# A hybrid decoder step on one core: background loads issued by GpSimd, and a planner that counts eight transfers in flight

## Chip, core and metric

The kernel runs on one core of one Trainium2 chip, as one launch. The metric is the device time of that launch in microseconds (us). GB/s and MB are decimal, KB are 1024 bytes.

## The reference, cut to what matters

A prompt of 512 positions and eight sample sequences of 8 positions (64 rows) run through the same two layers; all data are float32.

```python
# layer 0: attention and short convolution
hn = rms_norm(x, g)
q, k, v, z_a, gate_b, gate_c, h_in, z_b = split(hn @ w_in_ab, 8)      # 2048 -> 8192
o_a = dilated_attn(rotary(q), rotary(k), v) * silu(z_a)               # 8 heads of 128; the sample rows
                                                                      # read a cache of 2048 positions
o_b = gate_b * conv3(gate_c * h_in) * silu(z_b)
x = x + concat(o_a, o_b) @ w_out_ab
# layer 1: diagonal complex state space, 128 groups of 16 channels and 64 states
u, z = split(rms_norm(x, g) @ w_in_c, 2)
y = gelu(s5_scan(u, h0, lam, step, B, C) + d_skip * u)
y = y * sigmoid(y @ w_glu + b_glu) * silu(z)
x = x + y @ w_out_c
return rms_norm(x, final_norm), new keys, values, conv and state-space states
```

## The kernel before, in words

**The matrix products.** The 576 rows of activations stay in SBUF as two tiles, a_hi and a_lo, whose sum is the float32 value. A product is 120 jobs: 64 jobs of 128 output columns for w_in_ab (24 for the q, k and v of the heads, 8 for z_a, 32 for the convolution), 4 wide jobs of 512 columns for w_out_ab, 32 for w_in_c, 16 for w_glu, 4 wide ones for w_out_c. The weights come in halves of 512 KB (tile w, `load_half`, three buffers). ACT rounds a quarter of a half into wh, DVE takes the difference wl, and TensorE (PE) adds a_hi*wh, a_lo*wh and a_hi*wl into the PSUM tile mm.

**The background.** Beside the jobs run threads, which are Python generators: the turning of x into a_hi and a_lo (`x_turn`, `x_split`, `x_rows`), the prompt's attention (`prompt_head`), the tables of the state space (`ssm_setup`, `ssm_x`, `ssm_c`), the attention of the sample rows (`far_load`, `sample_far`, `near_load`, `sample_near`), the scan of layer 1, the stores and reloads between stages, and the final norm with the rows of h read again (`h_again`). In `ssm_x` the tiles E8 and B8 (512 KB each, one buffer each) are read from DRAM and DVE makes X8 of them (the trace names them E, B and X); `ssm_c` reads small rows of C (tile cn) and makes the tables Cs. In the sample's attention the near cache rows and all value rows come through tile kv (six buffers), the far key rows through tile kf (three buffers), 512 KB each; DVE multiplies kf by the query row qr and sums into fs, from which E is made that PE turns (tile tf). (Tile E of the sample's attention and tile E8 of the tables share a short name in the trace; the stretch tells them apart.)

**What sets the order.** All engines execute in program order, and that order is laid down when the program is built. A planner (`Clock`) keeps an estimated time for each engine and for each tile, from costs written into `Clock.op` and `Clock.cost`. Between two steps of a job, `between` calls `step`, which lets every background thread that is ready by these estimates (`could`) emit one piece of its instructions; a thread names the engine and the tiles that it waits for with `W(...)`. Loads are emitted in the same manner: a transfer stands in the queue of the engine that issues it (SP, ACT or POOL), behind whatever that engine was given earlier. Each transfer ends on one of eight counters, taken in turn: SP and ACT share one set of eight, POOL has another, and a transfer whose counter is still in use waits for that earlier one. In the kernel before, all weight loads and nearly all background loads stand on SP; POOL has the stores of intermediate results, a few fills and copies, and two of the five small rows of vr. The planner's cost of a transfer knows nothing of the eight counters.

Nearly every instruction is recorded by the helper `Engine`, so the trace gives line L215 for all of them (L218 after the change) and the tiles tell them apart.

Of the kernel before, what the change touches and what calls it, by code (L numbers as in the profile page):

```python
# [78 lines left out]
class Clock:  # L79


    def __init__(self):
        self.t = {e: 0.0 for e in ("PE", "ACT", "DVE", "POOL", "SP")}
        self.port = self.base = 0.0
        self.dma = 6500.0
        self.exact = False
        self.wr, self.rd = {}, {}
        self.row, self.ring, self.born, self.gone = {}, {}, {}, set()
        self.last = {}
        self.sbuf = set()  # L90
# [80 lines left out]
    def op(self, eng, op, a, k):  # L171
# [107 lines left out]
def hybrid_step(tc, I, O):  # L279
# [156 lines left out]
    def step():  # L436
        evacs()
        for _ in range(1):
            again = False
# [283 lines left out]
    ACT.dma_start(out=vr[48:64], in_=I["final_norm"].rearrange("(r p) -> r p", p=P))  # L723
    ACT.dma_start(out=vr[64:88], in_=I["conv_w"][0].rearrange("i (r p) -> (i r) p", p=P))
    POOL.memset(dr4, 0.0)
    POOL.memset(ssq, 1.0)

    def load_consts():
        SP.dma_start(out=cosr, in_=I["c_cos"])
        SP.dma_start(out=sinr, in_=I["c_sin"])  # L730
        SP.dma_start(out=sr, in_=I["state_conv"][0].rearrange("b i f -> (b i) f"))
        SP.dma_start(out=dr4[:, :, 0:GC], in_=I["d_skip"][0].rearrange("(q gi k) -> q gi k", gi=4, k=GC))
        SP.dma_start(out=pmask, in_=I["c_pmask"])
        SP.dma_start(out=fmask, in_=I["c_fmask"])
        SP.dma_start(out=eye, in_=I["c_eye"])

# [456 lines left out]
    def ssm_x(sp):  # L1193
        for c in range(G // CH):
            g0 = c * CH
            yield W("SP", e_scr, b_scr, slot=[(sp, "E8", 1), (sp, "B8", 1)])
            E = sp.tile([P, CH, 2, ST], F32, name="E8", tag="E8", bufs=1)
            B = sp.tile([P, CH, 2, ST], F32, name="B8", tag="B8", bufs=1)
            SP.dma_start(out=E.rearrange("p g a s -> p (g a s)"), in_=e_scr[:, g0:g0 + CH, :]
                         .rearrange("t g p -> t (g p)").unsqueeze(1).to_broadcast([T, GC, CH * P]))  # L1200
            SP.dma_start(out=B.rearrange("p g a s -> p (g a s)"), in_=b_scr[:, g0:g0 + CH, :]
                         .rearrange("k g p -> k (g p)").unsqueeze(0).to_broadcast([T, GC, CH * P]))
# [3 lines left out]
            for a, (p, q, f) in enumerate(((br, bi, sub), (bi, br, add))):  # L1206
# [11 lines left out]
    def ssm_c(sp, B0, PWT):  # L1218
# [3 lines left out]
        def load_cn(c):  # L1222
            if c < G // CH:
                g0 = c * CH
                x = cn[c] = sp.tile([P, 4, ST], F32, name="cn", tag="cn", bufs=2)
                for a, nm in ((0, "c_re"), (2, "c_im")):
                    SP.dma_start(out=x[:, a:a + 2, :], in_=I[nm][0, g0:g0 + CH].rearrange("g k p -> (g k) p")
                                 .unsqueeze(1).to_broadcast([P, 2, ST]))

        yield W("SP")  # L1230
        load_cn(0)
        for c in range(G // CH):
# [37 lines left out]
            if c % 2:  # L1270
                yield W("ACT", gsb)
                POOL.dma_start(out=gz_scr[(c - 1) * CH:(c + 1) * CH].rearrange("(q gi) k j -> (gi k) q j", gi=4)[:, :, 112:240],
                               in_=gsb)
# [99 lines left out]
    def far_load():  # L1373
        pp = sa["p"]
        for b in range(NB):
            for t in range(6):
                n = 6 * b + t
                if t == 0:
                    yield W("SP", q_scr, slot=[(pp, "qr", 1)], flag=lambda: sa["far"] >= n)
                    sa["qr"] = pp.tile([P, 1024], F32, name="qr", tag="qr", bufs=1)  # L1380
                    SP.dma_start(out=sa["qr"], in_=q_scr[b * 8:(b + 1) * 8].unsqueeze(0).to_broadcast([16, 8, 1024]))
                yield W("SP", slot=[(pp, "kf", 1)], flag=lambda: n - sa["far"] < 3 and n - 2 * sa["vload"] < 8)
                sa["kf"][n] = pp.tile([P, 1024], F32, name="kf", tag="kf", bufs=3)
                SP.dma_start(out=sa["kf"][n], in_=far_ap(ck, b, t))

# [42 lines left out]
    def near_load():  # L1428
        pp = sa["p"]
        for n, (f, c, b, t) in enumerate(near_seq):  # L1430
            yield W("SP", slot=[(pp, "kv", 1)], flag=lambda: n - sa["used"] < 6)
            x = sa["kv"][n] = pp.tile([P, 1024], F32, name="kv", tag="kv", bufs=6)
            SP.dma_start(out=x, in_=f(c, b, t))
            sa["vload"] = n + 1

    def sample_near():
# [3 lines left out]
        for pr in range(4):  # L1440
# [112 lines left out]
            yield from sample_out(pr, osb)  # L1553
        yield W("ACT", sa["oS"])
        POOL.dma_start(out=o_scr[0:8, :, NP:].rearrange("h p n -> p h n"), in_=sa["oS"])
        sa["done"] = True

    def open_sample():
# [6 lines left out]
        sa["oS"] = qs  # L1565
        SP.dma_start(out=sa["nmask"], in_=I["c_nmask"])
        SP.dma_start(out=sa["newmask"], in_=I["c_newmask"])
        sa["qz"] = pp.tile([P, 2, 2, 4, 32], F32, name="qz")
# [125 lines left out]
    def ev_z(n, ps):  # L1694
# [6 lines left out]
        stt(th, th, 1.0, zs, ALU.add, ALU.mult)  # L1701
        yield W("ACT", th)
        POOL.dma_start(out=z_scr[n], in_=th)
# [308 lines left out]
    def h_again():  # L2012
        yield W("SP")
        for i in range(5):
            for p0, p1, rows in pieces(i, h_scr[0:NP], h_scr[NP:NT]):
                yield W("SP", flag=lambda: cnt["done"] >= 116)
                SP.dma_start(out=fo["Y"][p0:p1, i, :] if i < 4 else fo["Ys"][p0:p1], in_=rows)
        fo["h"] = 4
        yield W("SP")
        SP.dma_start(out=fo["g"], in_=I["final_norm"].unsqueeze(0).to_broadcast([P, D]))  # L2020
        fo["gl"] = True
# [198 lines left out]
```

## Time and profile before

| | |
|---|---|
| time, median of 3 runs (lowest to highest) | 2281.84 us (2280.62 to 2285.08) |
| time of the profiled execution | 2286.27 us |
| its span, first to last instruction | 2284.4 us |
| mean granted TensorE clock | 0.986 |
| PE busy | 2183.2 us (96%) |
| DVE busy | 1263.7 us (55%) |
| ACT busy | 690.1 us (30%) |
| POOL busy | 117.9 us (5%) |
| queue of SP (q1) | 341.81 MB, 55.8% of the 16 DMA engines' span |
| queue of POOL (q0) | 40.50 MB, 5.4% |
| queue of ACT (q10) | 5.27 MB, 0.8% |

The time of an execution lies 1.87 us above its span. PE is the busy engine, so the time is what PE works, what it stands idle between instructions, and what it loses where its granted clock is 0.50 (1.2 GHz) in place of 1.00 (2.4 GHz). Idle time of the others counts where PE comes to wait for them.

### The profile page before, as it was taken

Reading aid. Unit: us, or ns where it says so; the run is one execution under the profiler, and the core shown is the slowest. Engines: PE = TensorE matmul, PEld = TensorE weight load, DVE = VectorE, ACT = ScalarE, POOL = GpSimd, SP = SyncE. Lnnn points to the kernel's source line nnn. Section 1 sums busy time; section 2 is a strip of 40 time slices with the busy share of each in tenths; the row PEclk is TensorE's granted clock in tenths of the full one; section 3 lists DMA queues with packets and bytes.
Section 4 is the critical chain, followed back from the end, with each engine's and each line's share of the span. In section 5 each row is a group of like instructions: output and inputs, shape, how many; then the busy total and the mean of one; then the engine's idle time right before and its main releaser. Section 6 shows DMA issues by size and latency. Waiting matters only on the chain. (4 is left out here: it accounts for less than half of the span.)

```text
span 2284.4 us, 38430 instructions
## 1 busy us (share of the span) xinstructions
PE 2183.2 (96%) x15581; PEld 2016.4 (88%) x15581; DVE 1263.7 (55%) x2380; ACT 690.1 (30%) x1400; POOL 117.9 (5%) x226
## 2 busy tenths in 40 slices
PE   5999999889989899999999999999999999999997
PEld 5999999889869789798977789999999999997785
DVE  2657778665845754333433352988894444443333
ACT  4453334332212213121332332222223333322222
POOL 0001111110000000000000000000002000000000
PEclk8999999999999999999999999999999999999999
DMA  5346678779999895857665435456645643338222
GB/s 165 99 135 168 194 196 216 194 196 275 235 259 248 201 278 149 261 128 204 188 207 158 130 119 157 131 184 204 177 140 173 188 121 105 107 106 213 74 65 83
DMA packets 391972, 390.03 MB, mean 171 GB/s; under 512 B 31260, under 2 KB 318340, under 8 KB 390452
## 3 DMA queue, kind: packets, MB, share of 16 engines
q1 hardware_dynamic: 370128, 341.81, 55.8%
q0 software_dynamic: 13120, 40.50, 5.4%
q10 hardware_dynamic: 8548, 5.27, 0.8%
q8 instruction: 122, 2.00, 0.4%
q14 instruction: 54, 0.44, 0.1%
HBM read 330.40 MB, written 65.51 MB: 173 GB/s over the span
## 5 line engine op out<-in xcount | busy, mean ns | idle before, releaser
L215 PE MATMUL mm<-a_hi,wh 128*128 128x288 f32 x3072 | 696.6, 308 | 11.2 <-ACT a_hi L215 6.9
L215 DVE TENSOR_TENSOR wl<-w,wh 128x512 fp32r<-128x512 f32 x576 | 393.3, 688 | 542.3 <-ACT wh L215 522.4
L215 PE MATMUL mm<-a_lo,wh 128*128 128x288 f32 x3072 | 662.0, 297 | 6.9 <-DVE a_lo L215 6.9
L215 PE MATMUL mm<-a_hi,wl 128*128 128x288 f32 x3072 | 662.8, 298 | 0.0
L215 PEld LDWEIGHTS mm<-a_hi,wh 128*128 128x128 f32 x3072 | 494.3, 191 | 60.6 <-issue 40.3
L215 ACT ACTIVATE wh<-w 128x512 fp32r<-128x512 f32 x576 | 357.1, 626 | 603.3 <-PE mm L215 320.8
L215 PEld LDWEIGHTS mm<-a_lo,wh 128*128 128x128 f32 x3072 | 498.4, 190 | 8.1 <-DVE a_lo L215 8.1
L215 PEld LDWEIGHTS mm<-a_hi,wl 128*128 128x128 f32 x3072 | 498.5, 190 | 0.0
L215 PE MATMUL mm<-y_lo,wh 128*128 128x288 f32 x512 | 109.7, 296 | 0.0
L215 PE MATMUL mm<-y_hi,wh 128*128 128x288 f32 x512 | 109.6, 296 | 0.0
L215 PE MATMUL mm<-y_hi,wl 128*128 128x288 f32 x512 | 109.6, 296 | 0.0
L215 PE MATMUL mm<-wh,a_hi 128*128 128x512 f32 x256 | 100.7, 393 | 5.1 <-DVE Y L215 4.3
L215 PE MATMUL mm<-wh,o_hi 128*128 128x512 f32 x256 | 101.4, 396 | 0.6 <-DVE h L215 0.6
L215 PE MATMUL mm<-wh,a_lo 128*128 128x512 f32 x256 | 100.2, 391 | 0.0
L215 PE MATMUL mm<-wl,a_hi 128*128 128x512 f32 x256 | 100.1, 391 | 0.0
L215 PE MATMUL mm<-wl,o_hi 128*128 128x512 f32 x256 | 99.9, 390 | 0.0
L215 PE MATMUL mm<-wh,o_lo 128*128 128x512 f32 x256 | 99.8, 390 | 0.0
L215 DVE TENSOR_TENSOR kf<-kf,qr 128x1024 f32<-128x1024 f32 x48 | 58.6, 1221 | 63.7 <-DMA kf<-cache_win_k 63.7
L215 PEld LDWEIGHTS mm<-y_hi,wh 128*128 128x128 f32 x512 | 82.5, 189 | 0.0
L215 PEld LDWEIGHTS mm<-y_lo,wh 128*128 128x128 f32 x512 | 82.5, 189 | 0.0
L215 PEld LDWEIGHTS mm<-y_hi,wl 128*128 128x128 f32 x512 | 82.5, 189 | 0.0
L215 ACT ACTIVATE S<-S,st 128x128 f32<-128x128 f32 (+3 forms) x64 | 35.0, 557 | 140.6 <-DVE st L215 140.4
(310 smaller groups left out, 2469.5 us busy)
## 6 DMA issues: line engine op xcount, KB each, us to landing
w<-w_in_ab SPq DMA_DIRECT2D x128, 512.0 KB
kv<-cache_win_v SPq DMA_DIRECT2D x80, 512.0 KB
w<-w_in_c SPq DMA_DIRECT2D x64, 512.0 KB
kf<-cache_win_k SPq DMA_DIRECT2D x48, 512.0 KB
kv<-cache_win_k SPq DMA_DIRECT2D x32, 512.0 KB
w<-w_out_ab SPq DMA_DIRECT2D x32, 512.0 KB
w<-w_glu SPq DMA_DIRECT2D x32, 512.0 KB
w<-w_out_c SPq DMA_DIRECT2D x32, 512.0 KB
```

What stands on the lines that cost most here:

```text
L215: r = f(*a, **k)
```

## The change

The issue of background loads moves from SP (and of three small rows from ACT) to POOL: the constants and the rows of vr, E8, B8 and cn, the cache rows kv, kf and qr with their masks, and the rows of h with the final gain (tile gf) at the end. Weight loads, the reads between stages (oa, ol, U, bx, cs, m0, z, y, x again) and a few others stay on SP. Some stores that POOL issued already name POOL instead of ACT in their `W(...)`. The planner takes a transfer to wait for the eighth before it on its set of counters, counts 600 ns in place of 900 for an issue by POOL and 1900 ns in place of 3200 from the last byte to the landing; and while fewer than two jobs are done, `step` goes round its threads up to three times.

```diff
@@ Clock.__init__ and Clock.op
+        self.lanes = {False: [0.0] * 8, True: [0.0] * 8}
         if op == "dma_start":
-            at = max(self.t[eng], t) + (370 if eng != "POOL" else 900)
+            lanes = self.lanes[eng == "POOL"]
+            at = max(self.t[eng], t, lanes.pop(0)) + (370 if eng != "POOL" else 600)
...
-            end = max(self.dma, at) + 3200
+            end = max(self.dma, at) + 1900
+            lanes.append(end)
@@ step
-        for _ in range(1):
+        for _ in range(3 if cnt["done"] < 2 else 1):
@@ vr rows and load_consts
-    ACT.dma_start(out=vr[0:16], in_=I["attn_norm"][0].rearrange("(r p) -> r p", p=P))
+    POOL.dma_start(out=vr[0:16], in_=I["attn_norm"][0].rearrange("(r p) -> r p", p=P))
...
-        SP.dma_start(out=cosr, in_=I["c_cos"])
+        POOL.dma_start(out=cosr, in_=I["c_cos"])
...
@@ ssm_x
-            yield W("SP", e_scr, b_scr, slot=[(sp, "E8", 1), (sp, "B8", 1)])
+            yield W("POOL", e_scr, b_scr, slot=[(sp, "E8", 1), (sp, "B8", 1)])
...
-            SP.dma_start(out=E.rearrange("p g a s -> p (g a s)"), in_=e_scr[:, g0:g0 + CH, :]
+            POOL.dma_start(out=E.rearrange("p g a s -> p (g a s)"), in_=e_scr[:, g0:g0 + CH, :]
...
-            yield W("ACT", X)
+            yield W("POOL", X)
@@ far_load, near_load
-                yield W("SP", slot=[(pp, "kf", 1)], flag=lambda: n - sa["far"] < 3 and n - 2 * sa["vload"] < 8)
+                yield W("POOL", slot=[(pp, "kf", 1)], flag=lambda: n - sa["far"] < 3 and n - 2 * sa["vload"] < 8)
...
-            SP.dma_start(out=x, in_=f(c, b, t))
+            POOL.dma_start(out=x, in_=f(c, b, t))
@@ h_again
-                SP.dma_start(out=fo["Y"][p0:p1, i, :] if i < 4 else fo["Ys"][p0:p1], in_=rows)
+                POOL.dma_start(out=fo["Y"][p0:p1, i, :] if i < 4 else fo["Ys"][p0:p1], in_=rows)
...
-        SP.dma_start(out=fo["g"], in_=I["final_norm"].unsqueeze(0).to_broadcast([P, D]))
+        POOL.dma_start(out=fo["g"], in_=I["final_norm"].unsqueeze(0).to_broadcast([P, D]))
```

**Order, tables of the state space.** SP before, late in the heads' stage (w is a weight half, E and B the rows of `ssm_x`, cn those of `ssm_c`, oa a reload of the prompt's attention):

```order
L215 DMA w<-w_in_ab 128x8x128 x2
L215 DMA E_4862<-e_scr 128x1x1024
L215 DMA B_4863<-b_scr 128x1x1024
L215 DMA oa<-oa_scr 128x512
L215 DMA w<-w_in_ab 128x8x128
L215 DMA cn<-c_re 128x2x64
L215 DMA cn<-c_im 128x2x64
L215 DMA w<-w_in_ab 128x8x128
```

POOL after the change, in the same stage:

```order
L218 DMA bx_scr<-X_3537 128x1024
L218 DMA E_3720<-e_scr 128x1x1024
L218 DMA B_3721<-b_scr 128x1x1024
L218 DMA cs_scr<-Cs 128x8x128
L218 DMA gz_scr<-gsb 128x4x128
L218 DMA cn<-c_re 128x2x64
L218 DMA cn<-c_im 128x2x64
L218 DMA bx_scr<-X_3812 128x1024
```

E and B no longer stand behind weight loads but behind the store of the X before them; on SP, 34 weight loads now follow each other there with nothing between.

**Order, cache rows of the sample's attention.** SP before, where the values of the second pair of sequences come:

```order
L215 DMA kf<-cache_win_k 128x1x1024
L215 DMA w<-w_in_ab 128x8x128
L215 DMA kv<-cache_win_v 128x1x1024
L215 DMA kf<-cache_win_k 128x1x1024
L215 DMA kv<-cache_win_v 128x1x1024
L215 DMA kf<-cache_win_k 128x1x1024
L215 DMA w<-w_in_ab 128x8x128
L215 DMA kv<-cache_win_v 128x1x1024 x2
L215 DMA w<-w_in_ab 128x8x128
L215 DMA qr<-q_scr 128x1x1024
```

POOL after the change, at that place (ncv and e are results of the convolution's jobs that go out):

```order
L218 DMA kf<-cache_win_k 128x1x1024
L218 DMA out_conv_p<-ncv 2x128
L218 DMA out_conv_s<-ncv 16x128
L218 DMA kv<-cache_win_v 128x1x1024
L218 DMA kf<-cache_win_k 128x1x1024
L218 DMA kv<-cache_win_v 128x1x1024
L218 DMA kf<-cache_win_k 128x1x1024 x2
L218 DMA kv<-cache_win_v 128x1x1024 x2
L218 DMA o_scr<-e_7835 128x576
L218 DMA kv<-cache_win_v 128x1x1024
```

The cache rows keep their order among themselves; their neighbours in the queue are now POOL's stores in place of the weights.

**Order, the first two jobs.** ACT before (a_hi is the turned x, wh a weight quarter, junk the square of x for the norm):

```order
L215 ACTIVATE a_hi<-xT,vec 128x512
L215 ACTIVATE a_hi<-xsg 128x8x64
L215 ACTIVATE a_hi<-xT,vec 128x512
L215 ACTIVATE junk,ssq<-xt 128x2048 x4
L215 ACTIVATE junk,ssq<-xs_t 64x2048
L215 ACTIVATE a_hi<-xT,vec 128x512 x2
```

ACT after the change, at that place:

```order
L218 ACTIVATE a_hi<-xsg 128x8x64
L218 ACTIVATE a_hi<-xT,vec 128x512
L218 ACTIVATE wh<-w 128x512
L218 ACTIVATE junk,ssq<-xt 128x2048
L218 ACTIVATE a_hi<-xT,vec 128x512
L218 ACTIVATE junk,ssq<-xt 128x2048 x3
L218 ACTIVATE junk,ssq<-xs_t 64x2048
L218 ACTIVATE a_hi<-xT,vec 128x512
```

One of the five squares now stands ahead of the next a_hi, and four stay together.

## Rows read from the trace of the kernel before

**Rows 1.** Busy time by stage: start, heads, sample's attention, last output product and end.

```profile
core 0: us, PE busy (x) PEld busy (x) DVE busy (x) ACT busy (x) POOL busy (x), PEclk, DMA share, GB/s
0.00:85.00 85.00, 59.98 (x392) 56.82 (x393) 32.20 (x62) 40.23 (x63) 2.21 (x11) 0.92 0.52 136
85.00:525.00 440.00, 420.06 (x3262) 403.65 (x3261) 314.87 (x692) 167.85 (x381) 63.41 (x102) 0.98 0.67 184
525.00:900.00 375.00, 350.39 (x2906) 315.28 (x2905) 232.51 (x320) 82.86 (x156) 10.98 (x31) 0.98 0.98 238
...
2055.00:2284.40 229.40, 211.66 (x905) 169.34 (x904) 75.66 (x143) 59.73 (x118) 0.00 (x0) 0.97 0.41 110
```

**Rows 2.** Timeline of PE, heads: the two longest waits of that stage.

```profile
447.29 1.11 PE L215 MATMUL pt<-ident,S 128*128 128x128 f32 x4 [3.99 <-ACT S L215]
...
503.87 1.12 PE L215 MATMUL pt<-ident,S 128*128 128x128 f32 x4 [4.71 <-ACT S L215]
```

**Rows 3.** Timeline of DVE ahead of the first of them.

```profile
439.96 0.69 DVE L215 TENSOR_TENSOR tb<-E,B 128x512 f32<-128x512 f32 x1 [8.17 <-DMA B<-b_scr]
```

**Rows 4.** Timeline of SP's queue ahead of the same wait.

```profile
415.23 9.01 SPq L215 DMA_DIRECT2D w<-w_in_ab  x2
424.30 0.60 SPq L215 DMA_DIRECT2D E<-e_scr  x1
```

**Rows 5.** Waits by waiting engine and releaser, 85 to 525: us in total, times, longest.

```profile
DVE tb L215 <- DMA B<-b_scr: 44.9, 13, 8.2
...
PE gp L215 <- DVE Cs L215: 8.1, 8, 1.5
```

**Rows 6.** Waits of SP's queue, 85 to 525.

```profile
SPq L215 <- DVE wl L215: 166.9, 33, 13.5
```

**Rows 7.** Busy time and granted clock right behind four waits of PE.

```profile
447.30:450.70 3.40, 3.40 (x15) 3.40 (x16) 3.37 (x8) 1.36 (x3) 0.00 (x0) 0.50 0.53 171
503.90:508.70 4.80, 4.80 (x21) 4.80 (x22) 3.35 (x5) 3.12 (x7) 0.55 (x1) 0.50 0.70 233
...
752.00:757.90 5.90, 5.88 (x26) 5.88 (x27) 5.83 (x7) 1.50 (x3) 0.00 (x0) 0.50 1.02 246
...
2110.80:2116.40 5.60, 5.56 (x10) 2.82 (x11) 2.49 (x5) 1.81 (x6) 0.00 (x0) 0.50 0.00 0
```

**Rows 8.** Waits of the sample's attention, 525 to 900.

```profile
DVE kf L215 <- DMA kf<-cache_win_k: 63.7, 24, 11.5
...
ACT wh L215 <- DMA w<-w_in_ab: 25.6, 7, 7.7
...
PE tf L215 <- DVE E L215: 9.4, 2, 8.1
```

**Rows 9.** Timeline of PE: two waits of that stage that go back to kf.

```profile
586.84 0.51 PE L215 MATMUL mm<-a_hi,wh 128*128 128x288 f32 x2 [4.32 <-DVE e L215]
...
752.02 0.87 PE L215 MATMUL tf<-ident,E 128*128 128x128 f32 x3 [8.11 <-DVE E L215]
```

**Rows 10.** DMA queues, 525 to 900: packets, MB, share of the 16 engines.

```profile
q1 hardware_dynamic: 62566, 86.72, 96.0%
```

**Rows 11.** DMA queues, 229 to 232: stores of POOL beside weight loads.

```profile
q1 hardware_dynamic: 867, 0.41, 54.4%
q0 software_dynamic: 94, 0.36, 45.8%
```

**Rows 12.** Groups of instructions on POOL: count, busy us, mean ns, idle before.

```profile
L215 POOL DMA_DIRECT2D bx_scr<-X x16 | 8.8, 551 | 64.2 <-DVE X L215 64.2
```

**Rows 13.** Timeline of the last output product: DVE, PE.

```profile
2108.30 1.29 DVE L215 TENSOR_TENSOR Y<-Y,gf 128x512 f32<-128x512 f32 x2 [4.68 <-DMA gf<-final_norm]
...
2110.84 0.79 PE L215 MATMUL mm<-wh,a_hi 128*128 128x512 f32 x1 [3.56 <-DVE Y L215]
```

**Rows 14.** Timeline of PE in the start.

```profile
32.57 0.85 PE L215 MATMUL mm<-a_lo,wh 128*128 128x288 f32 x2 [5.62 <-DVE a_lo L215]
...
53.20 0.85 PE L215 MATMUL mm<-a_hi,wh 128*128 128x288 f32 x2 [6.89 <-ACT a_hi L215]
```

More of the change, by code (lines that the diff above doesn't have):

```diff
@@ L718, in load_x @@
         SP.dma_start(out=xt[:, :, c * 256:(c + 1) * 256], in_=xsrc[:, :, c * 256:(c + 1) * 256])
-    ACT.dma_start(out=vr[0:16], in_=I["attn_norm"][0].rearrange("(r p) -> r p", p=P))
+    POOL.dma_start(out=vr[0:16], in_=I["attn_norm"][0].rearrange("(r p) -> r p", p=P))
     POOL.dma_start(out=vr[16:32], in_=I["ssm_norm"][0].rearrange("(r p) -> r p", p=P))
     POOL.dma_start(out=vr[32:48], in_=I["b_glu"][0].rearrange("(r p) -> r p", p=P))
-    ACT.dma_start(out=vr[48:64], in_=I["final_norm"].rearrange("(r p) -> r p", p=P))
-    ACT.dma_start(out=vr[64:88], in_=I["conv_w"][0].rearrange("i (r p) -> (i r) p", p=P))
+    POOL.dma_start(out=vr[48:64], in_=I["final_norm"].rearrange("(r p) -> r p", p=P))
+    POOL.dma_start(out=vr[64:88], in_=I["conv_w"][0].rearrange("i (r p) -> (i r) p", p=P))
     POOL.memset(dr4, 0.0)
@@ L728, in load_consts @@
     def load_consts():
-        SP.dma_start(out=cosr, in_=I["c_cos"])
[L730 to L735, printed above, removed]
+        POOL.dma_start(out=cosr, in_=I["c_cos"])
+        POOL.dma_start(out=sinr, in_=I["c_sin"])
+        POOL.dma_start(out=sr, in_=I["state_conv"][0].rearrange("b i f -> (b i) f"))
+        POOL.dma_start(out=dr4[:, :, 0:GC], in_=I["d_skip"][0].rearrange("(q gi k) -> q gi k", gi=4, k=GC))
+        POOL.dma_start(out=pmask, in_=I["c_pmask"])
+        POOL.dma_start(out=fmask, in_=I["c_fmask"])
+        POOL.dma_start(out=eye, in_=I["c_eye"])
     def vec_in():
@@ L1226, in load_cn @@
                 for a, nm in ((0, "c_re"), (2, "c_im")):
-                    SP.dma_start(out=x[:, a:a + 2, :], in_=I[nm][0, g0:g0 + CH].rearrange("g k p -> (g k) p")
+                    POOL.dma_start(out=x[:, a:a + 2, :], in_=I[nm][0, g0:g0 + CH].rearrange("g k p -> (g k) p")
                                  .unsqueeze(1).to_broadcast([P, 2, ST]))
-        yield W("SP")
+        yield W("POOL")
         load_cn(0)
@@ L1270, in ssm_c @@
             if c % 2:
-                yield W("ACT", gsb)
+                yield W("POOL", gsb)
                 POOL.dma_start(out=gz_scr[(c - 1) * CH:(c + 1) * CH].rearrange("(q gi) k j -> (gi k) q j", gi=4)[:, :, 112:240],
@@ L1378, in far_load @@
                 if t == 0:
-                    yield W("SP", q_scr, slot=[(pp, "qr", 1)], flag=lambda: sa["far"] >= n)
+                    yield W("POOL", q_scr, slot=[(pp, "qr", 1)], flag=lambda: sa["far"] >= n)
                     sa["qr"] = pp.tile([P, 1024], F32, name="qr", tag="qr", bufs=1)
-                    SP.dma_start(out=sa["qr"], in_=q_scr[b * 8:(b + 1) * 8].unsqueeze(0).to_broadcast([16, 8, 1024]))
-                yield W("SP", slot=[(pp, "kf", 1)], flag=lambda: n - sa["far"] < 3 and n - 2 * sa["vload"] < 8)
+                    POOL.dma_start(out=sa["qr"], in_=q_scr[b * 8:(b + 1) * 8].unsqueeze(0).to_broadcast([16, 8, 1024]))
+                yield W("POOL", slot=[(pp, "kf", 1)], flag=lambda: n - sa["far"] < 3 and n - 2 * sa["vload"] < 8)
                 sa["kf"][n] = pp.tile([P, 1024], F32, name="kf", tag="kf", bufs=3)
-                SP.dma_start(out=sa["kf"][n], in_=far_ap(ck, b, t))
+                POOL.dma_start(out=sa["kf"][n], in_=far_ap(ck, b, t))
     def sample_far():
@@ L1553, in sample_near @@
             yield from sample_out(pr, osb)
-        yield W("ACT", sa["oS"])
+        yield W("POOL", sa["oS"])
         POOL.dma_start(out=o_scr[0:8, :, NP:].rearrange("h p n -> p h n"), in_=sa["oS"])
@@ L1565, in open_sample @@
         sa["oS"] = qs
-        SP.dma_start(out=sa["nmask"], in_=I["c_nmask"])
-        SP.dma_start(out=sa["newmask"], in_=I["c_newmask"])
+        POOL.dma_start(out=sa["nmask"], in_=I["c_nmask"])
+        POOL.dma_start(out=sa["newmask"], in_=I["c_newmask"])
         sa["qz"] = pp.tile([P, 2, 2, 4, 32], F32, name="qz")
@@ L1701, in ev_z @@
         stt(th, th, 1.0, zs, ALU.add, ALU.mult)
-        yield W("ACT", th)
+        yield W("POOL", th)
         POOL.dma_start(out=z_scr[n], in_=th)
@@ L2012, in h_again @@
     def h_again():
-        yield W("SP")
+        yield W("POOL")
         for i in range(5):
             for p0, p1, rows in pieces(i, h_scr[0:NP], h_scr[NP:NT]):
-                yield W("SP", flag=lambda: cnt["done"] >= 116)
-                SP.dma_start(out=fo["Y"][p0:p1, i, :] if i < 4 else fo["Ys"][p0:p1], in_=rows)
+                yield W("POOL", flag=lambda: cnt["done"] >= 116)
+                POOL.dma_start(out=fo["Y"][p0:p1, i, :] if i < 4 else fo["Ys"][p0:p1], in_=rows)
         fo["h"] = 4
-        yield W("SP")
-        SP.dma_start(out=fo["g"], in_=I["final_norm"].unsqueeze(0).to_broadcast([P, D]))
+        yield W("POOL")
+        POOL.dma_start(out=fo["g"], in_=I["final_norm"].unsqueeze(0).to_broadcast([P, D]))
         fo["gl"] = True
```

4 lines of the change are left out of this document (2 added, 2 removed).

## Prediction

> **What bounds the kernel now.** I read the stages first [rows 1]. In the table, PE's idle time is a stage's length less its busy time, and the granted clock below 1.00 is work done at half speed. PE is idle for 25.0 us in the start (85.00 less 59.98), 19.9 in the heads' stage, 24.6 in the sample's attention and 17.7 in the last product and the end. The page gives PE 2183.2 us busy of a span of 2284.4, so all its idle time is 101 us: nothing that moves loads can save more than that, plus what the clock loses. Then I read PE's timeline for the waits themselves, and behind each the timeline of the engine that released it, until a load stood there.
>
> In the heads' stage the two longest waits are 3.99 and 4.71 us [rows 2], both for a softmax tile of ACT. Ahead of the first, DVE had sat 8.17 us for tile B [rows 3], and the queue of SP shows why B came late: two weight halves took 9.01 us to leave the queue and E stood behind them [rows 4]. That is a pattern: DVE waits for B 13 times, 44.9 us in all [rows 5], and SP's queue stands 33 times, 166.9 us in all, until DVE has freed a weight buffer [rows 6]. After such waits of PE the granted clock is 0.50, the lower of the two levels, for 3.4 and 4.8 us [rows 7].
>
> In the sample's attention DVE waits for the far key rows kf 24 times, 63.7 us, and ACT for weights 7 times, 25.6 us [rows 8]. PE's waits of 4.32 and 8.11 us [rows 9] follow on DVE's. But in this stretch SP's own queue holds the 16 DMA engines for 96.0% of the time [rows 10]. So a load may be late there because it was issued late, or because the engines are full; the view cannot tell them apart.
>
> **The change, part by part.**
>
> *Issue on POOL.* Moved are 3 vr rows, 7 constants, 32 loads of E and B, 32 of cn, 168 of kv, kf and qr, 2 masks, 20 pieces of h and one gf: 265 transfers. A 512 KB store in rows of 4 KB costs POOL 551 ns [rows 12]; 265 of them are 146 us beside POOL's 117.9, in 2284. POOL stays nearly empty, so the issue itself costs nothing; what counts is what stands behind what.
>
> *Heads, E and B.* They leave a queue that stood 166.9 us for weight buffers. On POOL they follow the store of the X before, which waits for the same DVE work that frees their buffers, so that store costs them nothing. Saved if both long waits go: 3.99 + 4.71 = 8.7 us of idle, and half of 3.4 + 4.8 us at the lower clock, 4.1: 12.8. Against it: DVE gets its table work earlier and closer together, and PE waits for Cs already, 8 times, 8.1 us [rows 5]; there are 16 chunks, so up to another 8.1. I take half, 4. Term: 9 us saved (bounds: 19.9 idle and 4.1 clock saved, 24; 8 lost).
>
> *Sample's attention.* The cache rows no longer stand behind weights that wait for a buffer, nor the weights behind the cache rows. If lateness is all issue, the whole 24.6 us of idle go, and up to 7.5 for the clock (0.98 over 375 us): 32. If it is all engines, nothing. How do two queues share an engine? The nearest row: between 229 and 232, while POOL stores 4 KB rows and SP loads weights in rows of 512 B, q0 has 45.8% and q1 54.4% of engine time, 0.36 and 0.41 MB [rows 11]. They share by bytes, so small weight rows are not starved. The 96.0% speaks for the end near nothing; I take a quarter of 32: 8 us saved. The Trainium skill (DMA: Bandwidth & Descriptors, section "Issuing engines are not separate DMA queues") says that transfers of all issuing engines interleave on the same 16 DMA engines, and that issuing from several saves only the issue time; by that this term would be nothing and the sum 2267. The 96.0% agrees with it; the waits of SP's queue for buffers are what it leaves out.
>
> *End.* DVE waits 4.68 us for gf, the last piece that SP issued after h, with an addition of Y behind it, and PE waits 3.56 us for that [rows 13], then runs 5.6 us at 0.50 [rows 7], which costs 2.8. On POOL gf follows only the pieces of h, without weights between, so it need only come 4.68 us earlier. I take 6 of the 6.4 (bounds: 6.4 saved; a Y that itself comes later, 4 lost).
>
> *Start.* PE's waits of 5.62 and 6.89 us [rows 14] go back to late weight halves and to ACT, which squares five rows of x in one piece. The constants leave SP ahead of a weight half, but their bytes then run beside x and the first weights; the first product of PE waits for vr, whose five rows now come from one queue, 3 more at 551 ns, 1.7 us. Of the five squares four still stand together in ACT's order, so the second wait stays. Term: 0 (bounds: 8 saved, 5 lost).
>
> *The planner.* What it gives is an order, and its matrix work is unchanged. In layer 1 and w_glu, no load of the path changes its queue: 0.
>
> Sum: 9 + 8 + 6 = 23 us saved. The profiled execution took 2286.27, so 2263.3; the median of the runs, 2281.84, lies 4.43 below that execution, which puts the changed kernel at **2259 us**, taken as the median of its runs. About 0.2% (4.6 us) is what can be told from no change.
>
> **The rivals.**
>
> A, the queue was everything: in the sample's attention all 32 us go in place of 8. For it: SP stands for weight buffers with cache rows behind. Against: the 96.0%. Time 2259 - 24 = 2235. Chance 0.14.
>
> B, the engines are the bound, and DVE is: sample 0, the heads' 12.8 given back by 16 waits on Cs (8.1), the end spared by only part of its 6.4. Between 2277 and 2282, say 2279. Chance 0.15.
>
> C, slower: the far key rows come later. On one queue a kf row waited for what was issued before it; on two, the weights that SP issues at once take up to half of the engines [rows 11] while 45 kf and many kv loads stand on POOL, behind each other, behind qr, which waits for DVE, and behind stores that wait for ACT. The place is DVE's product of kf and qr; DVE executes in order, with wl behind it. Price: today 63.7 us of DVE's waits go with 9.4 + 4.32 us of PE's, and 3 for the clock: 0.26 us for each us. If each of the 48 loads comes 2.65 us later (today's mean, 63.7 over 24), that is 127 us and 33 of PE's; with the 8 not saved, 2259 + 8 + 33 = 2300. It decides from 1.2 us a load: 58 us at 0.26 are the 15 that heads and end give. Chance 0.19.
>
> D, issue is blocked by DVE: each kf issue held for one DVE instruction of up to 1.2 us, 58 us, 15 of PE's; with the 8 not saved, 2282. Against: the 16 stores of 551 ns [rows 12] were issued while DVE was busy 315 of 440 us [rows 1]. The Trainium skill (SBUF — State Buffer, section "🔬 SBUF: two separate sides") states that GpSimd cannot write descriptors while VectorE runs a copy in its two-port mode; those 551 ns show no such hold. Chance 0.02.
>
> **How the numbers follow.** The forecast has 0.50, by itself 2245 to 2275. Faster by over 0.2%: forecast and A, 0.64. Within 0.2%: B and D, 0.17. Slower: C, 0.19. The range goes from A, 2234, to C's price, 2298; it leaves out half of C and the tail of A, some 0.15.
>
> **What would show it.** Right: DVE's waits for B in the heads' stage well below 44.9 us and the two waits of rows 2 gone; SP's queue holding little but weights; no wait for gf at the end; DVE's waits for kf at or below 63.7. B: q0 and q1 together above 95% of the engines between 525 and 900 with PE's idle time still near 24 us, and more waits on Cs. C: DVE's waits for kf above 120 us, and PE's waits for tf and os grown. The forecast is wrong if the start loses more than 5 us, or if PE comes to wait for a place that this list lacks, such as a store on POOL that frees a buffer late.

## The result, and the profile after

| | before | after the change |
|---|---|---|
| time, median (lowest to highest, 4 runs each) | 2283.38 us (2280.62 to 2285.08) | 2320.74 us (2318.71 to 2323.51) |
| time of the profiled execution | 2286.27 us | 2319.87 us |
| its span | 2284.4 us | 2318.1 us |
| PE busy, mean granted clock | 2183.2 us, 0.986 | 2195.6 us, 0.978 |
| POOL busy | 117.9 us | 263.9 us |

The ratio is 1.0166, with a 95% interval of 1.0148 to 1.0183: slower by 37 us, where 23 us less were forecast, and outside the range (2234 to 2298). PE works 12.4 us longer on the same 15581 instructions at a lower mean clock; the rest, 21.3 us, is idle time.

The first view is the busy time by stage (columns as in [rows 1]), after the change:

```profile
0.00:85.00 85.00, 61.88 (x420) 59.21 (x420) 36.99 (x82) 42.88 (x68) 7.39 (x21) 0.94 0.56 147
85.00:525.00 440.00, 409.15 (x3104) 389.58 (x3103) 306.29 (x665) 161.86 (x368) 104.12 (x155) 0.97 0.75 173
525.00:930.00 405.00, 364.76 (x2973) 329.61 (x2972) 235.05 (x318) 84.95 (x158) 79.95 (x170) 0.95 0.90 230
```

and the last of these stretches before:

```profile
525.00:930.00 405.00, 380.39 (x3130) 341.23 (x3129) 244.10 (x338) 91.46 (x170) 13.05 (x36) 0.98 0.96 232
```

PE's idle time is 23.1 us in the start (before 25.0), 30.9 in the heads' stage (19.9) and 40.2 in the sample's attention (24.6). So two stages lost, and the start did not.

A place in the work is better than a place in time to divide the loss. The rows of tile kf give one: the issue of the first far key row. In these lines the times after the colon are the least, median and longest issue in ns, then the start of the first and the last in us. Before:

```profile
L215 SPq DMA_DIRECT2D kf<-cache_win_k x48: 536/552/8268, 514.4 to 844.1; - x48
```

After:

```profile
L218 POOL DMA_DIRECT2D kf<-cache_win_k x48: 510/526/567, 533.2 to 888.5; - x48
...
DMA to landing us min/median/max: 4.8/11.1/19.8
```

The first cache row is issued 18.8 us later. From there to the end of the profiled executions it is 1771.9 us before and 1786.7 after, 14.8 more. The loss of 33.6 us thus has two parts: 18.8 by the end of the heads' stage, and 14.8 behind it, where the end had also been forecast to give 6. The division is rough, since another queue issues that row now. PE's own work gives a second one: its 3328 products of a_hi and wh come with the jobs, in one order. The kernel after the change is 24.6 us behind at the 901st of them (497.3 us in the kernel before), 43.1 behind at the 1651st (916.6 us), 39.7 at the 3001st (1821.4 us) and 33.7 at the 3151st (2124.3 us). By this, too, both stages lost, and the end gave 6.0 back.

**Heads.** The waits between 85 and 525 us (engine and tile that waited, releaser: us in total, times, longest) answer to [rows 5]:

```profile
DVE tb L218 <- DMA B<-b_scr: 66.4, 16, 6.9
...
PE gp L218 <- DVE Cs L218: 15.8, 16, 1.9
...
PE pt L218 <- ACT S L218: 7.7, 3, 3.7
```

DVE's waits for B did not fall but rose, from 44.9 to 66.4 us, at each of the 16 chunks, and PE waits for Cs 16 times in place of 8. The two waits of [rows 2] are gone from their places; three of the same kind, 7.7 us, stand elsewhere.

**Sample's attention.** The waits between 525 and 930 us answer to [rows 8]:

```profile
ACT wh L218 <- DMA w<-w_in_ab: 86.8, 11, 15.2
...
DVE kf L218 <- DMA kf<-cache_win_k: 38.9, 12, 8.4
...
PE to L218 <- DVE Ss L218: 13.6, 2, 6.9
...
PE tf L218 <- DVE E L218: 10.3, 2, 6.5
```

It is not the cache rows that come late now (DVE's waits for kf went from 63.7 to 38.9 us) but the weights: ACT waits 86.8 us for them, where it was 25.6. One of PE's new waits can be followed back through the timelines. PE:

```profile
715.01 1.12 PE L218 MATMUL to<-ident,Ss 128*128 128x128 f32 x4 [6.71 <-DVE Ss L218]
```

DVE, which makes Ss at 714.21, behind the rows that follow one wl in its order:

```profile
709.73 0.69 DVE L218 TENSOR_TENSOR wl<-w,wh 128x512 fp32r<-128x512 f32 x1 [11.30 <-ACT wh L218]
...
714.21 0.74 DVE L218 TENSOR_SCALAR Ss<-os,sst 128x512 f32<-128x512 f32 x1
```

ACT, whose wh waited for a weight half:

```profile
709.07 1.15 ACT L218 ACTIVATE wh<-w 128x512 fp32r<-128x512 f32 x2 [13.84 <-DMA w<-w_in_ab]
```

And SP, whose queue needed 28.88 us to let three halves go (between 680 and 720 us it waits 10.8 us for weight transfers issued before and 10.8 us for DVE's wl to free a buffer):

```profile
684.93 28.88 SPq L218 DMA_DIRECT2D w<-w_in_ab  x3
```

The DMA queues in 696 to 708 us and, as a second stretch with work on both, in 819 to 861 us (packets, MB, share of the 16 engines) show why:

```profile
q0 software_dynamic: 880, 3.20, 88.2%
q1 hardware_dynamic: 895, 0.45, 15.3%
...
q0 software_dynamic: 2948, 10.73, 89.1%
q1 hardware_dynamic: 2951, 1.49, 15.2%
```

POOL's queue (q0) and SP's (q1) got nearly the same number of packets, 880 and 895, then 2948 and 2951: one for one. But by the sizes in the trace most packets of q0 are 4096 B, a cache row, and nearly all of q1 are 512 B, a weight row. So in the first stretch the weights moved 0.45 MB while the cache moved 3.20.

**End.** In place of PE's wait of 3.56 us for Y behind gf [rows 13] there stands, between 2055 us and the end:

```profile
PE mm L218 <- DVE Y L218: 0.8, 1, 0.8
```

### The profile page after: what moved, and what is told of

It is laid out like the page before. It is cut to its first block, busy times and chain, and to the rows that moved or that the text cites. A ratio compares the mean times of both kernels' runs of the same rounds, so it can differ in the third digit from the quotient of the medians.

```text
span 2318.1 us, 38449 instructions
## 1 busy us (share of the span) xinstructions
PE 2195.6 (95%) x15581; PEld 2028.8 (88%) x15581; DVE 1265.1 (55%) x2380; ACT 688.7 (30%) x1400; POOL 263.9 (11%) x490
## 5 line engine op out<-in xcount | busy, mean ns | idle before, releaser
L218 PE MATMUL mm<-a_hi,wh 128*128 128x288 f32 x3072 | 704.4, 311 | 5.7 <-ACT a_hi L218 5.7
L218 PEld LDWEIGHTS mm<-a_hi,wh 128*128 128x128 f32 x3072 | 500.8, 193 | 58.7 <-issue 43.9
L218 DVE TENSOR_TENSOR kf<-kf,qr 128x1024 f32<-128x1024 f32 x48 | 58.5, 1219 | 39.0 <-DMA kf<-cache_win_k 38.9
## 6 DMA issues: line engine op xcount, KB each, us to landing
kf<-cache_win_k POOLq DMA_DIRECT2D x48, 512.0 KB, 11.1
kv<-cache_win_k POOLq DMA_DIRECT2D x32, 512.0 KB, 10.4
```

What stands on the lines that cost most here:

```text
L218: r = f(*a, **k)
```

## Experiments

Three suspects: the **landing time** of the planner (1900 ns, which puts DVE's work on E and B earlier in its order); the **tables' queue** (E, B and cn on POOL); the **cache's queue** (kv, kf and qr on POOL, Packets in the expectations). Ratios are against the kernel before, run beside it on the same chip; its median there was 2281 to 2285 us. Differences between two experiments are of their medians; the ratios put some of them up to 8 us elsewhere, and both are given where it matters. Idle time is PE's, as length less busy, between 85 and 525 us (heads) and between 525 and 930 (sample); the stages shift by up to 40 us between kernels, so the second reads only roughly.

### The planner's landing time

**plan_only**: the four planner hunks of the change, all loads on their old queues.

```diff
+            lanes = self.lanes[eng == "POOL"]
+            at = max(self.t[eng], t, lanes.pop(0)) + (370 if eng != "POOL" else 600)
...
+            end = max(self.dma, at) + 1900
+            lanes.append(end)
...
+        for _ in range(3 if cnt["done"] < 2 else 1):
```

> The kernel before with the change's planner alone (eight transfers in flight, 600 and 1900 ns, three rounds in the first two jobs); every load stays on its old queue. Theory Packets (with work on both queues a DMA engine takes a packet of each in turn, so weight rows of 512 B get through one for every 4 KB row of POOL; the loss is the queue's): weights and cache rows stand in one queue again, so 2283 us, within 8. Theory Planner (1900 ns is too short, so instructions that wait for a load are put too early in their engine's order; the loss is the order's): 2305 us or more, with DVE's waits for B near the 66.4 us of the change.

2299.44 us, ratio 1.0060 (1.0039 to 1.0082). Waits for B 66.2 us, as Planner said; the time is between the two. About two fifths of the loss, 14.7 of 37 us, is there without one moved load, and it lies in the heads: 31.8 us of idle time there, against 19.9 before; in the sample's attention it is 26.6, near the 24.6 before.

**landing_only**: one number.

```diff
-            end = max(self.dma, at) + 3200
+            end = max(self.dma, at) + 1900
```

> The kernel before with one number of the planner changed: 1900 ns in place of 3200 from the last byte to the landing. Theory Landing (DVE's work on each of the 16 chunks of E and B is put 1.3 us earlier in its order, and DVE executes in order): DVE's waits for B between 85 and 525 go from 44.9 to about 66 us (16 times 1.3 is 21), PE's idle time there from 20 to about 30, time 2292 to 2302 us. Rival (the count of eight transfers or the rounds shape the heads' order): waits for B near 45 us, 2275 to 2288 us.

2312.15 us, ratio 1.0138 (1.0110 to 1.0165): slower even than expected. Its row of the stage table and its waits, 85 to 525:

```profile
85.00:525.00 440.00, 401.06 (x3040) 380.81 (x3039) 301.96 (x672) 157.43 (x359) 59.51 (x89) 0.96 0.64 170
```

```profile
DVE tb L215 <- DMA B<-b_scr: 69.0, 13, 9.5
```

One number of the planner doubles the heads' idle time (19.9 to 38.9 us) and adds 24.1 us to the waits for B; 16 chunks at 1.3 us are 20.8.

**planner_3200**: plan_only with 3200.

> The kernel before with the change's planner except the landing time, which stays 3200 ns. Theory Landing: DVE's waits for B near 45 us and PE's idle time in the heads near 20 us again, the start keeps the 5 us that the planner alone gave: 2272 to 2284 us. Rival (count of eight, 600 ns or rounds are to blame): waits for B near 66 us, PE idle over 28 us in the heads, 2293 us or more.

2275.18 us, ratio 0.9958 (0.9938 to 0.9978). Waits for B 41.9, heads' idle time 18.8, start's 19.9. The count of eight, the 600 ns and the rounds are not to blame; the start keeps its 5 us.

**rounds_and_end**: before, with the three rounds and `h_again` on POOL.

> The kernel before with two parts of the change alone: three rounds in the first two jobs, and the rows of h and gf issued by POOL. If parts add as the stages show them: the start gives 5 us, the end 6, nothing else moves: 2266 to 2276 us. Rival (each new order of the background costs or gives some us at random, so a gain in the start is not kept): 2278 to 2292 us.

2264.30 us, ratio 0.9926 (0.9904 to 0.9948), 1.7 us under the range. Both parts are gains, but they are not all of the 19 us: the start gives 4 us of idle time and the end 5.0 (by the products of a_hi and wh), while the sample's attention, where nothing was to move, has 19.3 us in place of 24.6.

**rounds_end_4500**: that kernel, with 4500.

```diff
-            end = max(self.dma, at) + 3200
+            end = max(self.dma, at) + 4500
```

> The kernel with three rounds and the end's loads on POOL (2264.3 us), and 4500 ns in place of 3200 from the last byte to the landing: the same step as the change made, in the other direction. Theory Landing: DVE's waits for B fall by up to 21 us from 44.5, PE's idle time in the heads from 18.7 to about 14: 2255 to 2263 us. Rival (3200 is long enough; later work only crowds something else): waits for B above 38 us, or the time 2264 to 2276 us.

2254.36 us, ratio 0.9873 (0.9852 to 0.9894), just under the range and the lowest median of all. Stage and waits, 85 to 525:

```profile
85.00:525.00 440.00, 432.78 (x3468) 417.93 (x3467) 324.35 (x677) 170.18 (x384) 63.09 (x102) 1.00 0.72 198
```

```profile
DVE tb L215 <- DMA B<-b_scr: 22.6, 11, 3.8
...
PE gp L215 <- DVE Cs L215: 2.8, 3, 1.5
```

The step that cost in one direction pays in the other: waits for B are 69.0 us at 1900 (landing_only), 44.9 and 44.5 at 3200 (before, rounds_and_end) and 22.6 at 4500; idle time 38.9, 19.9 and 18.8, and 7.2.

**rounds_end_6000**: 6000 in the same place.

> The kernel with 4500 ns (2254.36 us) with 6000 ns. If 4500 has taken what there was to take (7.2 us of idle time in the heads, 22.6 us of DVE's waits for B): waits for B go on to 10 us or less, but the time stays within 2250 to 2260 us. Rival (loads are placed too late, other tables come late in turn): 2262 us or more.

2278.17 us, ratio 0.9973 (0.9957 to 0.9989): the rival was right. Heads' idle time goes on to 2.8 us and waits for B to 13.6, but the sample's attention has 33.9, over half of it in one wait on the timeline of PE:

```profile
572.78 1.54 PE L215 MATMUL tf<-ident,E 128*128 128x128 f32 x6 [17.91 <-DVE E L215]
```

Of the four values tried, 4500 is the best; at 6000 the tables are early but the next stage is crowded.

**change_3200**: the whole change, with 3200.

> The whole change with the landing time put back to 3200 ns. Theory Landing: the heads' stage is back at about 20 us of PE's idle time, DVE's waits for B there fall below 66 us, the sample's attention keeps its loss; start and end keep their gain: 2283 to 2297 us. Rival (landing time and queues cost together, each through the other, so the order is not the heads' trouble once POOL issues): heads' idle time stays near 30 us, 2303 to 2322 us.

2289.78 us, ratio 1.0026 (1.0009 to 1.0044), as Landing said: from 1.0166 to 1.0026 by one number, 32 us. Heads' idle time is 23.9 us and the waits for B 54.9; the sample's attention keeps 37.3 us, with 74.5 us of ACT's waits for weights. So 1900 in place of 3200 cost 28 us alone, 24 with the change's planner (plan_only against planner_3200) and 31 in the whole change.

### The queue of E, B and cn

**tables_on_sp**: the change with E, B and cn on SP; the order of PE, DVE and ACT is unchanged.

```diff
-            POOL.dma_start(out=E.rearrange("p g a s -> p (g a s)"), in_=e_scr[:, g0:g0 + CH, :]
+            SP.dma_start(out=E.rearrange("p g a s -> p (g a s)"), in_=e_scr[:, g0:g0 + CH, :]
...
```

> The change with E, B and cn issued by SP again; the order of PE, DVE and ACT is then the same, instruction for instruction, as in the change, so only the queues differ. Theory Packets: on POOL these rows stand behind stores of 512 KB and share the engines with the weights, which is what makes B late; 2305 to 2314 us, DVE's waits for B between 85 and 525 well below 66.4 us. Theory Planner (the heads' loss is the order's): 2317 to 2330 us, DVE's waits for B at 66 us or above.

2313.46 us, ratio 1.0114 (1.0091 to 1.0136), 7 us below the change (12 by the ratios) and clear of its interval. Waits for B, 85 to 525, against 66.4:

```profile
DVE tb L218 <- DMA B<-b_scr: 56.9, 14, 8.3
```

With the order held still, POOL's queue makes B later, not earlier.

**without_both**: the change with 3200 and with kv, kf, qr and the masks on SP.

> The change without its two suspects: landing time 3200 ns, and kv, kf, qr and the masks issued by SP; constants, E, B, cn, the rows of h and gf stay on POOL, the count of eight and three rounds stay. If Landing and Packets are the whole loss, what is left is the start's and the end's gain: 2266 to 2279 us. Rival (E, B and the constants on POOL cost by themselves): 2284 us or more.

2286.15 us, ratio 1.0020 (1.0004 to 1.0036): expected 2266 to 2279, a miss. Something else cost some 14 us.

**start_back**: that, with the vr rows and constants on ACT and SP again.

> The kernel without both suspects (2286.15 us) and with the five vr rows and the seven constants issued by ACT and SP again, as before. If these loads on POOL are what eats the start's gain (PE waits 12.2 us for vr there, 9.4 in the planner with 3200 ns alone): PE's idle time in the first 85 us from 24.7 to 20, 2279 to 2283 us. Rival (the start's order, not the queue, lost it): idle 24 us or more there, 2284 us or more. If the whole 14 us that are open lie here, 2268 to 2274 us.

2285.27 us, ratio 1.0016 (1.0001 to 1.0032). The start's idle time goes from 24.5 to 21.5 us and PE's wait for vr from 12.2 to 10.0, so these loads do eat most of the rounds' gain. The other kernels agree: of those with three rounds, the seven with these loads on POOL have 22.6 to 24.9 us of idle time in the start, the seven with them on ACT and SP 19.4 to 21.5. But the heads have 26.3 us in place of 21.1, so the time stays. The 14 us are not there.

**tables_back**: without_both, with E, B and cn on SP.

> The kernel without both suspects (2286.15 us) and with E, B and cn issued by SP again. If the tables' loads on POOL are what is left of the loss: DVE's waits for B between 85 and 525 from 49.7 to about 42 us, PE's idle time in the sample's attention from 30.0 to about 22: 2268 to 2277 us. Rival (the residue belongs to the order that this planner makes, whichever queue issues them): 2282 us or more.

2265.78 us, ratio 0.9897 (0.9877 to 0.9917): 20 us (28 by the ratios), and more than expected. Waits for B from 49.7 to 36.9, first cache row from 514.3 to 506.8 us, sample's idle time from 30.2 to 23.6.

**tables_alone**: before, with only E, B and cn on POOL (and the `W("POOL", ...)` of their stores).

> The kernel before with E, B and cn issued by POOL, and nothing else. Theory Behind the store (on POOL E and B follow the 512 KB of the X before them in one queue, and share the engines with the weights): DVE's waits for B between 85 and 525 from 44.9 to about 60 us, 2286 to 2296 us. My prediction's step (they leave a queue that waits for weight buffers) would have waits for B well below 44.9 us and 2270 to 2276 us.

2315.86 us, ratio 1.0110 (1.0086 to 1.0135), worse than either expectation. Waits for B rose to 58.7 us as expected; the heads' idle time did not rise (19.6), but the first cache row comes at 531.9 us, 17.5 later. Its sample's attention and the wait that dominates it:

```profile
525.00:930.00 405.00, 358.69 (x2904) 317.54 (x2902) 235.32 (x321) 83.84 (x158) 13.84 (x39) 0.95 0.94 232
```

```profile
612.98 0.90 PE L215 MATMUL tf<-ident,E 128*128 128x128 f32 x3 [15.96 <-DVE E L215]
```

The tables end later (last product of E and B at 521 us, before 500), the cache rows start behind them, and PE, in its order, comes to the turning of E (tile tf) before the key rows it is made of are there. Both runs put E and B on another queue, and the planner makes another order of that. So the 20 to 28 us of tables_back and the 25 to 31 of tables_alone are queue and order together; the 7 to 12 of tables_on_sp are the queue by itself.

Why B is late on POOL, the change's POOL timeline suggests:

```profile
476.34 0.55 POOL L218 DMA_DIRECT2D bx_scr<-X  x1 [7.61 <-DVE X L218]
476.88 0.63 POOL L218 DMA_DIRECT2D E<-e_scr  x1
477.51 0.61 POOL L218 DMA_DIRECT2D B<-b_scr  x1
```

The issue is prompt. But the 512 KB of the store stand ahead of the 1 MB of E and B in one queue, and B lands 12.0 us after its issue (median of 16). How much of the 12.0 is the store and how much the weights beside it was not tried.

### The queue of the cache rows

**queue_only**: all queues of the change, planner of before.

> The change's queues with the planner of before (no count of transfers, 900 and 3200 ns, one round). Theory Packets: ACT still waits for weights over 60 us between 525 and 930, and the time is 2300 to 2325 us. Theory Planner: ACT's waits for weights fall to about 26 us as before, and the time is 2260 to 2285 us.

2295.47 us, ratio 1.0047 (1.0028 to 1.0067): under the lower end that Packets gave. ACT's waits for weights 92.3 us and the sample's idle time 36.9, as it said. That it is faster than tables_alone, which moves less, says that the parts do not add.

**cache_on_sp**: the change with kv, kf, qr and the masks on SP.

> The change with kv, kf, qr and the two masks issued by SP again. Theory Packets: the loss of the sample's attention (15.6 us of PE's idle time and about 12 of clock) comes back, ACT's waits for weights there fall from 86.8 to about 26 us: 2290 to 2300 us. Theory Planner: the short landing time still places those instructions too early: 2312 to 2325 us.

2306.11 us, ratio 1.0095 (1.0057 to 1.0134). ACT's waits for weights fall to 16.2 us as Packets said, but PE's idle time only from 40.2 to 34.4 and the time by 15 us, not by 20 to 30. And without_both, the same move under 3200, gains nothing that can be told from change_3200 (1.0020 against 1.0026). So the starving of the weights is there each time, 74.5 to 92.3 us in the four kernels with whole rows on POOL (the change, queue_only, tables_on_sp, change_3200) against 10.4 to 38.5 in those with them on SP, but its price depends on the order. Both moves also make another order of PE, DVE and ACT, and with the rows on SP, DVE waits for kf instead (74.0 us in cache_on_sp).

**cut_512**: queue_only with tiles of 8 x 132 floats for kv and kf.

```diff
-            x = sa["kv"][n] = pp.tile([P, 1024], F32, name="kv", tag="kv", bufs=6)
+            x = sa["kv"][n] = pp.tile([P, NH, 132], F32, name="kv", tag="kv", bufs=6)[:, :, 0:P]
```

> The queue-only kernel (POOL issues, planner of before) with the rows of kv and kf landing in pieces of 512 B (tiles of 8 x 132 instead of 1024 floats a row); every engine's order stays the same, instruction for instruction, and the bytes too. Theory Packets (an engine takes a packet of each queue in turn): weights then get one 512 B packet for each 512 B of POOL, ACT's waits for weights between 525 and 930 fall from 92.3 us to under 45, PE's idle time there from 36.9 to under 30: 2278 to 2290 us. Rival Full (the engines are simply full, so weights are late whatever the size): ACT's waits stay at 80 us or more, 2290 to 2310 us.

2336.37 us, ratio 1.0236 (1.0206 to 1.0267), worse than both. The queues, 525 to 930, of queue_only:

```profile
q0 software_dynamic: 19312, 69.25, 65.4%
q1 hardware_dynamic: 47884, 24.90, 26.1%
```

and of cut_512:

```profile
q0 software_dynamic: 18670, 66.92, 72.1%
q1 hardware_dynamic: 42129, 21.91, 25.5%
```

The edit did not do what it was for: q0's packets stayed as large (by the sizes in the trace 16038 of the 18670 are still 4096 B; nearly all others are 4 B), and each took longer, 0.721 x 16 x 405 / 18670 = 250 ns in place of 219. ACT's waits for weights grew from 92.3 to 133.2 us and the sample's idle time from 36.9 to 62.4. POOL's issue of a kf load also took 878 ns at the median in place of 524. Longer turns of q0 would do this to q1, but Full says the same, so it does not tell the two apart.

**half_rows**: queue_only with each load of kv and kf issued as two.

```diff
-            POOL.dma_start(out=x, in_=f(c, b, t))
+            for hf in (0, 512):
+                POOL.dma_start(out=x[:, hf:hf + 512], in_=f(c, b, t)[..., hf:hf + 512])
```

> The queue-only kernel with every load of kv and kf issued as two transfers of half rows (packets of 2 KB in place of 4); the planner counts the pair as the one load it was, so PE, DVE, ACT and SP keep their order. Theory Packets: weights get one 512 B packet for each 2 KB of POOL while both queues are full, about twice their share; ACT's waits for weights between 525 and 930 fall from 92.3 to 60 us or less, PE's idle time there from 36.9 to 31 or less: 2280 to 2291 us. Rival Full (weights are late because the engines are full, whatever the size of a packet): ACT's waits 80 us or more, 2292 to 2305 us.

2272.88 us, ratio 0.9949 (0.9931 to 0.9967): 22 us faster than queue_only, with ACT's waits at 56.8 us and idle time at 17.3. The numbers are those of Packets or better, but the reason given is not what happened. The queues, 525 to 930:

```profile
q0 software_dynamic: 22505, 73.33, 64.7%
q1 hardware_dynamic: 51481, 26.71, 27.6%
```

Half rows as packets would have nearly doubled q0's 19312; it has 3193 more, of which 2193 are of 4 B and 918 of 4096 B. What did change is that POOL now waits for its own transfers:

```profile
POOL kv L218 <- DMA kv<-cache_win_v: 14.7, 21, 1.9
...
POOL kv L218 <- DMA kf<-cache_win_k: 12.1, 22, 1.3
```

43 times in these two rows, 10 times in queue_only, and a half of kf lands 8.3 us after its issue, where a whole one took 11.4. With eight counters, eight halves are 2 MB in flight instead of 4. The two traces agree: between 525 and 930 us POOL never has more than eight transfers between issue and landing, and the rows of kv, kf and qr among them are at most 4.2 MB in queue_only (2.0 on average) and 2.4 MB in half_rows (1.3). So the weights meet a shorter line. That fits the gain, but was not tried by itself.

**change_3200_halves**: the whole change, with 3200 and half rows.

> The whole change with the landing time at 3200 ns (2289.78 us) and the loads of kv and kf in half rows of 2 KB, all still on POOL. Theory Packets: the sample's attention gets back what half rows gave under the planner of before (22 us): ACT's waits for weights there from 74.5 to under 50 us, PE's idle time from 37.4 to about 20: 2266 to 2276 us, faster than before. Rival (that gain came from that one order): idle 30 us or more there, 2282 us or more.

2268.08 us, ratio 0.9939 (0.9917 to 0.9961): 22 us below change_3200 (20 by the ratios), with PE, DVE and ACT in the same order. ACT's waits are 28.0 us, idle time 16.4. The whole change, its queues untouched, becomes a gain by one number and by half rows.

**best_of_both**: rounds_end_4500 with kv, kf, qr and masks on POOL, in half rows.

> The kernel before with three rounds in the first two jobs, 4500 ns of landing time, the end's loads on POOL (2254.36 us so far), and kv, kf, qr and the masks on POOL, kv and kf in half rows. If the two findings add: the heads as in the kernel with 4500 ns (7 us of PE's idle time), the sample's attention at or below its 17.4 us: 2245 to 2255 us. Rival (with POOL's queue the later placed work crowds, or weights are short again): PE's idle time in the sample's attention 22 us or more, 2258 us or more.

2256.53 us, ratio 0.9885 (0.9862 to 0.9907), between the two expectations and within the uncertainty of rounds_end_4500 (0.9873). PE's idle time in the sample's attention is 15.8 us (17.6 there), though ACT waits 61.5 us for weights. The findings do not add: half rows on POOL beat whole rows on POOL in the two kernels above, but not the rows on SP here.

## Why the prediction was wrong, step by step

In short: the forecast saved 9 + 8 + 6 us and put the planner at 0. The planner's landing time alone takes 28 to 31 us, the first two terms have the wrong sign, and only the end came as forecast.

**What bounds the kernel**: right. The waits named (for B, Cs, kf and the weights) are the ones that moved.

**Issue on POOL, 0**: right. 265 transfers at 551 ns were to add 146 us of busy time to POOL; it has 263.9 in place of 117.9, 146.0 more, and no wait of PE, DVE or ACT in the profile ends on an instruction of POOL.

**The planner, 0**: wrong, and the largest error. "What it gives is an order, and its matrix work is unchanged": the order is the price. DVE executes in order, so a product of E and B that stands 1.3 us too early in 16 chunks holds back the softmax and Cs behind it: DVE's waits for B go from 44.9 to 69.0 us and PE's idle time in the heads from 19.9 to 38.9. Alone this costs 28 us (landing_only), and undoing it in the change gives 31 (change_3200). The trace could have warned: B's 44.9 us of waits [rows 5] already said that the estimate was too short, and the change made it shorter.

**Heads, 9 saved**: wrong in sign. "That store costs them nothing" looked at when E and B are issued and not at the bytes ahead of them in their new queue. They lost the wait behind weights and now stand behind a store, beside the weights: 7 to 12 us lost with the order held still, 20 to 31 with the order that follows. Which of the two makes B late is not shown. The half of 8.1 us that was set against the gain for Cs came nearly whole (15.8 against 8.1).

**Sample's attention, 8 saved**: wrong in sign. "They share by bytes, so small weight rows are not starved" was read from [rows 11], where q0 had 94 packets in 3 us and q1 867. POOL's store was in work through that window (issued at 227.93 us, landed 6.0 us later), but the counts fit two queues on different engines: 94 packets in 45.8% of 16 engines' time are about 7 engines busy with q0 at any moment (an estimate), and the rest had rows of q1 alone. Nor were those packets all weights: by size 570 of the 867 are weight rows of 512 B. The window showed no turns on one engine. With work of both queues on every engine it is packet for packet, 880 and 895, or 2948 and 2951. The Trainium skill (DMA: Bandwidth & Descriptors, section "Queues, rings and completion order") says that an engine goes round the queues that have work and finishes a whole packet of one, typically 9 to 17 descriptors, before it switches. The trace agrees with turns that do not look at bytes; how many descriptors one of its packets holds it does not show. That the weights starve is shown. The price in time is 15 us in one order (cache_on_sp) and too little to tell in another (without_both); with the order held still, half rows gave back 22 us twice.

**End, 6 saved**: right, in mechanism and size. PE's wait for Y is 0.8 us in place of 3.56, and the lag of PE's products falls from 39.7 to 33.7 us there.

**Start, 0**: near the truth by luck, as a sum of two that cancel. The forecast gave the rounds nothing; they give 4 to 5 us of idle time (25.0 to 21.1 in rounds_and_end, 19.9 in planner_3200). The vr rows and constants on POOL, put at 1.7 us, take most of it back (24.5 in without_both, 21.5 when they are moved back).

**The rivals.** A fell. B had the waits on Cs right, 16 times, but not the engines: between 525 and 900 us q0 and q1 together have 91.8%, less than the 95% that it named, and PE's idle time rose. C, 2300, had the sign and the stage, but the wrong victim: DVE's waits for kf fell below 63.7 us instead of passing 120, and it was the weights that came late. D fell: kf issues take 526 ns at the median and 567 at most. The sentence that came true is the last one of the prediction: PE came to wait for a place that the list lacked, here Ss behind wl behind a weight half.

**What stays open**: whether half rows help because fewer bytes are in flight, how much of the tables' 20 to 31 us is order, and why the price of the cache's queue depends so much on the order.

## What to carry to other kernels

In a kernel whose order is fixed from estimates, an estimate of when a load has landed is a tuning number with a price at every in-order engine: try it in both directions before judging anything built on it (here 1900, 3200, 4500 and 6000 ns gave 1.0138 alone, and 0.9926, 0.9873, 0.9973 with two small edits). Before moving loads to a second queue, look at what stands ahead of them in bytes there, and at the row size on either side: large rows on one queue hold back small rows on the other. And read how two queues share only from a stretch in which both have work on the same engines (their shares of the 16 engines there add up to over 100%, 88.2% and 15.3%).

## What the runs showed of the hardware that was not expected

- Two queues with work got packets one for one (880 and 895 in 12 us, 2948 and 2951 in 42 us), so 3.20 MB and 0.45 MB of bytes in the first stretch.
- A load of 512 KB issued by POOL landed a median of 11.1 us (kf) and 12.0 us (B) after its issue.
- POOL's queue showed packets of 4096 B whether a cache row landed whole (16608 of 19312 in queue_only), in pieces of 512 B that lie 16 B apart (16038 of 18670 in cut_512), or was issued in halves of 2 KB (17526 of 22505 in half_rows). In pieces a packet took 250 ns on average in place of 219, and POOL's issue of a load 878 ns in place of 524.
